# A decoder block in split single precision: two weight slabs of the projections exchange their ways of being multiplied, VectorE writes the diagonal matrices of the norms, and the FFN output's activations are split pair by pair

## The chip, the cores and the metric

The kernel runs on one core of a Trainium2 chip. The time is the device time of one execution in microseconds (us). Three runs of the kernel before took 939.85 us in the median (938.61 to 940.29). A further execution was recorded by the hardware profiler: it took 939.93 us, and its trace spans 937.8 us, so that 2.1 us lie around the span.

The five engines that matter are TensorE (PE in the profile, with PEld for its weight loads), VectorE (DVE), ScalarE (ACT), GpSimd (POOL) and SyncE (SP), which issues the transfers of the weights. Each carries out its own instructions in the order in which they stand in its queue; semaphores hold an instruction back until what it reads has been written and what it overwrites has been read.

## The reference

The input is x, 512 tokens of 1024 channels, with 16 meta tokens set before them (528 in all). Cut to its steps:

```python
u = rmsnorm(h, mix_norm_w)
q, k, v, g_ret, lru_in, lru_gate, gate_a, gate_b = split(u @ w_in)   # 1024 -> 8192
o = chunk_retention(rotary(q), rotary(k) * 128**-0.5, v)             # 8 heads of 128
o = o * rsqrt(mean(o * o) + eps)
y_ret = (silu(g_ret) * o) @ w_branch_ret
y_lru = (gelu(lru_gate) * rg_lru(conv(lru_in))) @ w_branch_lru
h = h + (sigmoid(gate_a) * y_ret + sigmoid(gate_b) * y_lru) @ w_out
u = rmsnorm(h, ffn_norm_w)
g, up = split(u @ w_ffn_in)                                          # 1024 -> 2 x 2816
h = h + (silu(g) * up) @ w_ffn_out                                   # 2816 -> 1024
return rmsnorm(h, final_norm_w)[:, 16:]
```

## The kernel before

All activations lie in SBUF; the weights are streamed from HBM once, in quarters ("pieces") of 128x512 numbers. Products are made in single precision from two halves: ScalarE casts a piece to `hi` (line 290), VectorE, for some pieces GpSimd, subtracts it from the piece and has `lo` (line 294, `low`). A product is three matmuls, hi x hi, hi x lo and lo x hi (lines 360 to 364, and 372 to 374 in `block`). Activations are split in the same way (`split`, lines 418 to 422: cast on line 421, subtraction on line 422).

A slab of weights (1024 input channels by 256 outputs) is multiplied in one of two ways. "Plain" takes eight blocks of twelve matmuls straight from the four pieces. "The scheme" (`fast`, lines 376 to 400) takes seven blocks, from pieces and from four sums of pieces that GpSimd makes (`combine`, lines 257 to 261: s1, s3, s2, s4, with the addition on line 260). So it casts and subtracts seven operands instead of four, and between its blocks it needs copies of PSUM by ScalarE (`ws` line 392, `pz` 394, `u2` 398) and one addition by VectorE (`pz` line 393), on whose result a later block on the same bank waits; at the end VectorE adds the parts (lines 407 and 408, for keys line 813). `PLAIN_R` (line 68) lists which slabs of queries (Q), keys (K) and ret gates (G) of the four pairs of heads, 0 to 3, are plain. In the trace the banks of a scheme carry its name: `zwg` and `yxg` are the two banks of a ret gate, `zwf` and `yxf` of an FFN input slab, `zwq` and `yxq` of a query slab; plain ones are named by the slab alone (`k`, `f`).

Pieces live in rings: 8 raw quarters (`RAW`), 4 sums (`SUMS`), 9 pairs hi and lo (`RING`). A piece is loaded when a slot is free.

Before each of the two large projections the rows are normed and transposed. `rms_factors` (lines 480 to 491) takes the mean square of a tile of 128 tokens (ScalarE, line 484), adds the epsilon (`rv`, GpSimd, line 476), raises it to the power -1/2 (`rr`, GpSimd, line 477) and writes the factor onto the diagonal of a 128x128 matrix (line 490, on GpSimd before the change). TensorE multiplies the tile with this diagonal (line 523), which norms and transposes it at once. The first norm has the tiles x0 to x3 (banks `uT`), the second the tiles h0 to h3 (banks `hT`); h0 and h1 go without a diagonal, by a row scale of VectorE (line 1123). VectorE then multiplies by the norm's weights (line 508), ScalarE casts (511), VectorE subtracts (513).

The first norm's order on the engines is written out by hand (`FIRST_STEPS`, lines 47 to 49). Everywhere else a scheduler in the compiler decides the order on each engine from its own model of durations; what the program states first has the higher priority. `behind` (line 239) adds an edge of order without a semaphore: with it each `combine` stays behind the diagonal last written on GpSimd.

The FFN has 22 slabs of input (`w_fi`, two plain, then a loop from `FIRST` to `NJ` with `fast512` and the gate `ffn_gate`), whose gated outputs are kept in `F`, eleven tiles of 128x1024, two slabs in each. The output projection (`w_fo`) walks over k = 0 to 21 and both halves of the outputs, with eight banks `fo`. `operand(i)` splits `F[i]`; before the change it is defined behind the input loop and is called for three tiles ahead at each k.

Of the kernel before, what the change touches and what calls it, by code (L numbers as in the profile page):

```python
# [11 lines left out]
F32R = mybir.dt.float32r  # L12
# [52 lines left out]

PLAN = "R0 R1 R2 R3 A0 A1 A2 A3 I0 I1 BR T0 L0 I2 T1 L1 I3 L2 T2 B0 L3 T3 B1 B2 B3 BL"

PLAIN_R = "K0 G0 K1 K2 K3".split()
NORM = 2.0
SUM = 2.0  # L70

# [39 lines left out]
class Slots:  # L111
# [28 lines left out]
    def put(self, *tiles):  # L140
        for t in tiles:
            _, slot, i = self.held.pop(id(t))
            if i is None:
                self.free.append(slot)
                continue
            slot[2] -= 1
            self.halves.append((slot, i))
            if slot[2] == 0:
                self.halves = [h for h in self.halves if h[0] is not slot]
                self.free.append(slot[0])  # L150
# [3 lines left out]
def hybrid_block(ctx: ExitStack, tc: tile.TileContext, a: dict):  # L154
# [84 lines left out]
    def behind(ins, other):  # L239

        if other is not None:
            tc.add_manual_dep(ins.ins, other.ins.name, mybir.DependencyInfo(
                mybir.DependencyClass.NoSync, mybir.DependencyReason.DATA), reason="issue order")
        return ins
# [12 lines left out]

    def combine(key, i, name, x, y, op):
        sums[key, i, name] = wpool.tile([P, Q4], F32, tag="sum", bufs=SUMS, name=f"{name}_{key}{i}")
        behind(nc.gpsimd.tensor_tensor(sums[key, i, name], x, y, op=op), state.get("diag"))  # L260
        return sums[key, i, name]

    def emit(n, later=False):
# [155 lines left out]
    def split(p, src, engine=nc.vector):  # L419
        hi, lo = p  # L420
        nc.scalar.copy(hi, src)  # L421
        engine.tensor_tensor(lo, src, hi.bitcast(F32), op=ALU.subtract)
# [57 lines left out]
    def rms_factors(src, name, parts=P, diagonal=True):  # L480

        scratch = get(D)
        ssq = small.tile([P, 1], F32, tag="ssq", bufs=4, name=f"ssq_{name}")
        nc.scalar.activation(scratch[:parts], src, AF.Square, accum_out=ssq[:parts])
        put(scratch)
        r = rsqrt_mean(ssq[:parts], D, 1, name, parts, engine=nc.gpsimd)
        if not diagonal:
            return r
        diag = get(P)
        state["diag"] = nc.gpsimd.tensor_scalar_mul(diag[:parts, :parts], ident[:parts, :parts], r)  # L490
        return diag


# [690 lines left out]
    token_half(1)  # L1184
    finish(item)
    put(*VX.pop("b12"))
    for j in range(FIRST, NJ):
        gu = get(D)
        fast512("w_fi", j, VV, gu, "f")
        ffn_gate(j, gu[:, :SEQ], gu[:, SEQ:])  # L1190
        for b in ("t1", "t3", "b21", "b11", "b22", "t4", "t2") if j == NJ - 1 else ():
            put(*VX.pop(b))
        put(gu)
# [40 lines left out]


    acc = [[bank(f"fo{t}_{hf}") for hf in range(2)] for t in range(NC_)]
    parts = {}

    def operand(i):

        if i < len(F) and i not in parts:
            parts[i] = get(D, F32R), get(D, F32R)
            split(parts[i], F[i])
            put(F[i])

    def token_tile(t, k, hf, w, start, stop):
        fh, fl = (p[:, k % 2 * SEQ + t * C:k % 2 * SEQ + (t + 1) * C] for p in parts[k // 2])
        mm3(acc[t][hf], fh, fl, *w, start, stop)

    ws = {}  # L1250
    for k in range(NJ - LAST_K):
        for i in range(k // 2, k // 2 + 3):
            operand(i)
        for hf in range(2):
            ws[k, hf] = weights(("w_fo", k // 2, k % 2 + 2 * (1 - hf)))[0]
            for t in range(NC_):
                token_tile(t, k, hf, ws[k, hf], k == 0, False)
        if k % 2 == 1:
            put(*parts.pop(k // 2))
    ks = range(NJ - LAST_K, NJ)  # L1260
# [71 lines left out]
```

## Time and profile before

| | us |
|---|---|
| median of 3 runs | 939.85 |
| profiled execution | 939.93 |
| its span | 937.8 |
| TensorE busy | 918.5 |
| VectorE busy | 681.3 |
| ScalarE busy | 464.4 |
| GpSimd busy | 343.0 |

TensorE is the engine to read first. Matmuls overlap in the trace: one of 256 columns is listed with some 0.28 us, but the next starts 0.12 us after it, so stretches are read by the starts. "Idle before" in square brackets at the end of a row is how long the engine stood still before the instruction, with what released it. [...]

### The profile page before, as it was taken

Reading aid. Unit: us, or ns where it says so; the run is one execution under the profiler, and the core shown is the slowest. Engines: PE = TensorE matmul, PEld = TensorE weight load, DVE = VectorE, ACT = ScalarE, POOL = GpSimd, SP = SyncE. Lnnn points to the kernel's source line nnn. Section 1 sums busy time; section 2 is a strip of 40 time slices with the busy share of each in tenths; the row PEclk is TensorE's granted clock in tenths of the full one; section 3 lists DMA queues with packets and bytes.
Section 4 is the critical chain, followed back from the end, with each engine's and each line's share of the span. In section 5 each row is a group of like instructions: output and inputs, shape, how many; then the busy total and the mean of one; then the engine's idle time right before and its main releaser. Section 6 shows DMA issues by size and latency. Waiting matters only on the chain.

```text
span 937.8 us, 16991 instructions
## 1 busy us (share of the span) xinstructions
PE 918.5 (98%) x6598; PEld 862.8 (92%) x6598; DVE 681.3 (73%) x912; ACT 464.4 (50%) x823; POOL 343.0 (37%) x247
## 2 busy tenths in 40 slices
PE   8999999999999999999999999999999999999996
PEld 8999999998999889999998888999999999788885
DVE  5877977888788836777745428999999999832223
ACT  6653454554555336847833314655555556722213
POOL 5234634445350002102200215587887885000003
PEclk9999999999999999999999999999999999999998
DMA  7142123131224332233442222132333234422202
GB/s 278 46 135 84 54 95 109 38 111 50 64 87 129 113 102 82 77 113 101 136 135 91 94 75 89 52 118 93 101 107 121 91 100 127 143 92 96 84 1 90
DMA packets 48496, 91.48 MB, mean 98 GB/s; under 512 B 5520, under 2 KB 5648, under 8 KB 48416
## 3 DMA queue, kind: packets, MB, share of 16 engines
q1 hardware_dynamic: 46976, 86.70, 28.6%
q10 hardware_dynamic: 1440, 3.71, 1.2%
q8 instruction: 51, 0.84, 0.3%
q14 instruction: 29, 0.24, 0.1%
HBM read 88.29 MB, written 2.10 MB: 96 GB/s over the span
## 4 chain that ended last, share of the span: by engine, by line
PE 90%; DVE 5%; DMA 2%; issue 2%; ACT 1%; POOL 1%; POOLq 0%; DVEq 0%; SPq 0%; ACTq 0%
PE fo L362 4%; PE fo L364 4%; PE fo L363 4%; PE zwf L372 4%; PE zwf L373 4%; PE zwf L374 4%; DVE lo L294 3%; PE yxf L372 3%; PE yxf L374 3%; PE yxf L373 3%; PE lg L374 2%; PE gate L374 2%; PE gate L372 2%; PE lg L372 2%; PE lg L373 2%
## 5 line engine op out<-in xcount | busy, mean ns | idle before, releaser
L294 DVE TENSOR_TENSOR lo<-raw_w_in,hi 128x512 fp32r<-128x512 f32 x99 | 84.7, 861 | 36.9 <-ACT hi L290 34.8
L372 PE MATMUL zwf<-b,hi 128*128 128x256 f32 x320 | 90.8, 285 | 1.8 <-DVE pzf L393 1.8
L290 ACT CAST hi<-raw_w_in 128x512 fp32r<-128x512 f32 x99 | 60.7, 620 | 63.8 <-PE w_br L363 13.8
L373 PE MATMUL zwf<-b,hi 128*128 128x256 f32 x320 | 89.6, 280 | 0.0
L374 PE MATMUL zwf<-b,lo 128*128 128x256 f32 x320 | 89.5, 280 | 0.0
L294 DVE TENSOR_TENSOR lo<-s_w_fi,hi 128x512 fp32r<-128x512 f32 x80 | 83.7, 1083 | 1.3 <-ACT hi L290 0.8
L294 DVE TENSOR_TENSOR lo<-raw_w_fo,hi 128x512 fp32r<-128x512 f32 x44 | 30.3, 690 | 64.7 <-ACT hi L290 64.7
L260 POOL TENSOR_TENSOR s_w_fi<-raw_w_fi,raw_w_fi 128x512 f32<-128x512 f32 x40 | 69.0, 1743 | 8.2 <-DVE lo L294 8.2
L362 PE MATMUL fo<-hi,b 128*128 128x512 f32 x176 | 69.6, 395 | 0.4 <-ACT b L421 0.4
L363 PE MATMUL fo<-lo,b 128*128 128x512 f32 x176 | 69.1, 393 | 0.0
L364 PE MATMUL fo<-hi,b 128*128 128x512 f32 x176 | 68.1, 393 | 0.0
L294 DVE TENSOR_TENSOR lo<-raw_w_fi,hi 128x512 fp32r<-128x512 f32 x46 | 67.7, 1500 | 0.0
L372 PE MATMUL yxf<-b,hi 128*128 128x256 f32 x240 | 65.5, 281 | 2.1 <-ACT pzf L394 2.1
L374 PE MATMUL yxf<-b,lo 128*128 128x256 f32 x240 | 66.7, 281 | 0.0
L373 PE MATMUL yxf<-b,hi 128*128 128x256 f32 x240 | 66.6, 280 | 0.0
L372 PEld LDWEIGHTS zwf<-b,hi 128*128 128x128 f32 x320 | 60.0, 188 | 4.3 <-DVE pzf L393 4.1
L290 ACT CAST hi<-raw_w_fo 128x512 fp32r<-128x512 f32 x44 | 27.3, 621 | 73.1 <-PE fo L364 71.4
L294 DVE TENSOR_TENSOR lo<-s_w_in,hi 128x512 fp32r<-128x512 f32 x52 | 50.6, 976 | 14.4 <-ACT hi L290 12.1
L374 PEld LDWEIGHTS zwf<-b,lo 128*128 128x128 f32 x320 | 60.4, 189 | 0.0
L373 PEld LDWEIGHTS zwf<-b,hi 128*128 128x128 f32 x320 | 60.3, 189 | 0.0
L290 ACT CAST hi<-s_w_fi 128x512 fp32r<-128x512 f32 x80 | 48.1, 617 | 20.8 <-PE zwf L373 15.0
L290 ACT CAST hi<-raw_w_fi 128x512 fp32r<-128x512 f32 x68 | 41.6, 619 | 33.0 <-PE yxf L373 18.2
(380 smaller groups left out, 3277.2 us busy)
## 6 DMA issues: line engine op xcount, KB each, us to landing
raw_w_in<-in_w_in SPq DMA_DIRECT2D x112, 256.0 KB, 3.1
raw_w_fi<-in_w_fi SPq DMA_DIRECT2D x88, 256.0 KB, 3.3
raw_w_fo<-in_w_fo SPq DMA_DIRECT2D x44, 256.0 KB, 2.9
raw_w_v<-in_w_v SPq DMA_DIRECT2D x16, 256.0 KB, 4.3
raw_w_br<-in_w_br SPq DMA_DIRECT2D x16, 256.0 KB, 3.3
raw_w_bl<-in_w_bl SPq DMA_DIRECT2D x16, 256.0 KB, 3.1
raw_w_out<-in_w_out SPq DMA_DIRECT2D x16, 256.0 KB, 2.9
b<-in_x SPq DMA_DIRECT2D x4, 512.0 KB, 6.3
```

Of the source, the lines that this page charges most:

```text
L260: behind(nc.gpsimd.tensor_tensor(sums[key, i, name], x, y, op=op), state.get("diag"))
L290: nc.scalar.copy(hi, src)
L294: engine.tensor_tensor(lo, src, hi.bitcast(F32), op=ALU.subtract)
L362: nc.tensor.matmul(out, wh, xh, start=start, stop=False, skip_group_check=True)
L363: nc.tensor.matmul(out, wh, xl, start=False, stop=False, skip_group_check=True)
L364: nc.tensor.matmul(out, wl, xh, start=False, stop=stop, skip_group_check=True)
L372: nc.tensor.matmul(out, wh, xh, start=start and i == 0, stop=False, skip_group_check=True)
L373: nc.tensor.matmul(out, wh, xl, start=False, stop=False, skip_group_check=True)
L374: nc.tensor.matmul(out, wl, xh, start=False, stop=i == 3, skip_group_check=True)
```

## The change

`PLAIN_R` takes the keys of pair 2 off the list and puts the ret gate of pair 3 on it: K2 (264 columns per block) goes from plain to the scheme, G3 (256 columns) from the scheme to plain. The diagonal of `rms_factors` is written by VectorE, and the edge of order between diagonals and sums is gone. `operand` is defined ahead of the FFN input loop; the tile 0 is split before the last input slab is stated, the others behind the first half of each k, one at a time, and two tiles ahead of their use at most.

```diff
-PLAIN_R = "K0 G0 K1 K2 K3".split()
+PLAIN_R = "K0 G0 K1 K3 G3".split()
...
-        behind(nc.gpsimd.tensor_tensor(sums[key, i, name], x, y, op=op), state.get("diag"))
+        nc.gpsimd.tensor_tensor(sums[key, i, name], x, y, op=op)
...
-        state["diag"] = nc.gpsimd.tensor_scalar_mul(diag[:parts, :parts], ident[:parts, :parts], r)
+        nc.vector.tensor_scalar_mul(diag[:parts, :parts], ident[:parts, :parts], r)
...
+    parts = {}
+    def operand(i):
+        if i < NJ // 2 and i not in parts:
+            parts[i] = get(D, F32R), get(D, F32R)
+            split(parts[i], F[i])
+            put(F[i])
     for j in range(FIRST, NJ):
+        if j == NJ - 1:
+            operand(0)
         gu = get(D)
         fast512("w_fi", j, VV, gu, "f")
...
     for k in range(NJ - LAST_K):
-        for i in range(k // 2, k // 2 + 3):
-            operand(i)
         for hf in range(2):
             ws[k, hf] = weights(("w_fo", k // 2, k % 2 + 2 * (1 - hf)))[0]
             for t in range(NC_):
                 token_tile(t, k, hf, ws[k, hf], k == 0, False)
+            if hf == 0:
+                operand((k + 1) // 2 + 1)
```

How the change moves instructions is shown at three places, before and after, by the order in which they stand in an engine's queue.

The first place is VectorE at the start of the program. `lo4` and `lo5` are weight pieces of the values, `uT1` and `uT2` the transposed tiles x1 and x2, `b20` the diagonal. Before:

```order
L294 TENSOR_TENSOR lo2_182<-raw_w_v0_2_128,hi2_181 128x512
L508 TENSOR_TENSOR b7_111<-uT1_1_202,vec_70 128x4x128
L508 TENSOR_TENSOR b6_110<-uT1_0_207,vec_70 128x4x128
L513 TENSOR_TENSOR b13_117<-b7_111,b12_116 128x4x128
L513 TENSOR_TENSOR b11_115<-b6_110,b10_114 128x4x128
L294 TENSOR_TENSOR lo4_264<-raw_w_v0_1_261,hi4_263 128x512
L294 TENSOR_TENSOR lo5_270<-raw_w_v1_1_267,hi5_269 128x512
```

With the change:

```order
L294 TENSOR_TENSOR lo2_182<-raw_w_v0_2_128,hi2_181 128x512
L490 TENSOR_SCALAR b20_148<-ident_82,rr_x2_198 128x128
L508 TENSOR_TENSOR b7_111<-uT1_1_202,vec_70 128x4x128
L508 TENSOR_TENSOR b6_110<-uT1_0_207,vec_70 128x4x128
L513 TENSOR_TENSOR b13_117<-b7_111,b12_116 128x4x128
L513 TENSOR_TENSOR b11_115<-b6_110,b10_114 128x4x128
L490 TENSOR_SCALAR b20_148<-ident_82,rr_x3_247 128x128
L294 TENSOR_TENSOR lo4_264<-raw_w_v0_1_261,hi4_263 128x512
L294 TENSOR_TENSOR lo5_270<-raw_w_v1_1_267,hi5_269 128x512
```

Two diagonals stand in the queue now: that of x2 (`rr_x2`) ahead of the two multiplications of tile x1, that of x3 ahead of `lo4` and `lo5`.

The second place is GpSimd at the second norm, around the factor of h3 (`rv_h3`, `rr_h3`). `s1_w_fi2` to `s4_w_fi2` are the sums of FFN input slab 2, `s1_w_fi3` the first of slab 3, `lo232` and `lo236` pieces of the plain slabs 0 and 1. Before:

```order
L294 TENSOR_TENSOR lo232_6681<-raw_w_fi0_1_6678,hi232_6680 128x512
L294 TENSOR_TENSOR lo236_6733<-raw_w_fi1_1_6730,hi236_6732 128x512
L476 TENSOR_SCALAR rv_h3_6743<-ssq_h3_6741 128x1
L477 TENSOR_TENSOR rr_h3_6744<-rv_h3_6743,mhalf_78 128x1
L490 TENSOR_SCALAR b176_6747<-ident_82,rr_h3_6744 128x128
L260 TENSOR_TENSOR s1_w_fi2_6753<-raw_w_fi2_0_6749,raw_w_fi2_1_6751 128x512
L260 TENSOR_TENSOR s3_w_fi2_6757<-raw_w_fi2_2_6755,raw_w_fi2_0_6749 128x512
L260 TENSOR_TENSOR s2_w_fi2_6759<-s1_w_fi2_6753,raw_w_fi2_2_6755 128x512
```

With the change:

```order
L294 TENSOR_TENSOR lo232_6675<-raw_w_fi0_1_6672,hi232_6674 128x512
L260 TENSOR_TENSOR s1_w_fi2_6747<-raw_w_fi2_0_6743,raw_w_fi2_1_6745 128x512
L294 TENSOR_TENSOR lo236_6727<-raw_w_fi1_1_6724,hi236_6726 128x512
L260 TENSOR_TENSOR s3_w_fi2_6751<-raw_w_fi2_2_6749,raw_w_fi2_0_6743 128x512
L260 TENSOR_TENSOR s2_w_fi2_6753<-s1_w_fi2_6747,raw_w_fi2_2_6749 128x512
L476 TENSOR_SCALAR rv_h3_6737<-ssq_h3_6735 128x1
L260 TENSOR_TENSOR s4_w_fi2_6757<-raw_w_fi2_3_6755,s2_w_fi2_6753 128x512
L260 TENSOR_TENSOR s1_w_fi3_7014<-raw_w_fi3_0_7010,raw_w_fi3_1_7012 128x512
L477 TENSOR_TENSOR rr_h3_6738<-rv_h3_6737,mhalf_78 128x1
```

Before, the factor of h3 and its diagonal stand directly behind the two `lo` and ahead of all sums; now the four sums of slab 2 and the first of slab 3 stand ahead of `rr_h3`. On TensorE the order there is the same in both: the transposes `hT2`, 24 matmuls of `f0`, then `hT3`, which reads the diagonal of h3.

The third place is the passage from the last FFN input slab (21) to the output, on TensorE. `yxf21` is a bank of that slab, `zwf21` the other. Before, the end of one block of `yxf21` and the start of the next, which reads the sum s2 (`hi376`) and follows on the same bank once ScalarE has copied it (`pzf21`, line 394):

```order
L372 MATMUL yxf21_9746<-b161_6353,hi373_9653 128x256
L373 MATMUL yxf21_9746<-b162_6354,hi373_9653 128x256
L374 MATMUL yxf21_9746<-b161_6353,lo373_9654 128x256
L372 MATMUL yxf21_9746<-b181_6947,hi376_9704 128x256
L373 MATMUL yxf21_9746<-b182_6948,hi376_9704 128x256
```

With the change:

```order
L372 MATMUL yxf21_9744<-b161_6347,hi373_9647 128x256
L373 MATMUL yxf21_9744<-b162_6348,hi373_9647 128x256
L374 MATMUL yxf21_9744<-b161_6347,lo373_9648 128x256
L362 MATMUL fo0_0_9884<-hi377_9716,b215_9738 128x512
L363 MATMUL fo0_0_9884<-lo377_9717,b215_9738 128x512
L364 MATMUL fo0_0_9884<-hi377_9716,b216_9739 128x512
```

Behind the block that ends with `lo373`, 29 matmuls of the output (`fo0_0` to `fo3_0`, and some of `fo0_1` and `fo1_1`) stand now, ahead of the next block of `zwf21`. The operand they read, `b215` and `b216`, is `F[0]`. On ScalarE the cast of `F[0]` (line 421, out of `b183`) has moved too. Before:

```order
L394 COPY pzf21_9748<-yxf21_9746 128x256
L320 ACTIVATE b214_9741<-b213_9615 128x512
L421 CAST b235_10434<-b211_9470 128x1024
L290 CAST hi383_9845<-raw_w_fo1_3_9843 128x512
L421 CAST b231_10282<-b205_8900 128x1024
L398 COPY u2f21_9749<-yxf21_9746 128x256
L290 CAST hi384_9863<-raw_w_fo1_1_9861 128x512
L421 CAST b217_9894<-b183_6960 128x1024
```

With the change:

```order
L290 CAST hi369_9556<-s2_w_fi20_9439 128x512
L421 CAST b215_9738<-b183_6954 128x1024
L290 CAST hi370_9588<-s1_w_fi21_9576 128x512
L392 COPY wsf20_9612<-zwf20_9610 128x256
L290 CAST hi371_9615<-s3_w_fi21_9580 128x512
L290 CAST hi372_9631<-raw_w_fi21_3_9584 128x512
```

`b217<-b183` (before) and `b215<-b183` (now) are the cast of `F[0]`. Before, it comes behind the last slab's `pzf21` and `u2f21` and behind casts of other tiles of `F`; now it comes ahead of the first operand of the last slab, `hi370`. On TensorE the waiting block of `yxf21` is no longer the next in the queue.

## Rows read from the trace of the kernel before

**Rows 1.** The page's head and its first part: the span, and each engine's busy time, its share and its number of instructions.

```profile
span 937.8 us, 16991 instructions
...
PE 918.5 (98%) x6598; PEld 862.8 (92%) x6598; DVE 681.3 (73%) x912; ACT 464.4 (50%) x823; POOL 343.0 (37%) x247
```

**Rows 2.** All waits of TensorE, grouped: what waited, for whose result, in total, how often, and the longest. Groups that are not used are left out.

```profile
PE uT L523 <- POOL b L490: 2.7, 1, 2.7
PE zwg L372 <- DVE pzg L393: 2.2, 1, 2.2
PE yxf L372 <- ACT pzf L394: 2.1, 2, 1.9
PE zwf L372 <- DVE pzf L393: 1.8, 3, 0.8
...
PE v L363 <- DVE lo L294: 0.7, 1, 0.7
...
PE fo L362 <- ACT b L421: 0.4, 1, 0.4
```

**Rows 3.** TensorE's timeline around the ret gate of pair 3: start, duration, engine, line, operation, number; in brackets the idle time before it and what ended it.

```profile
220.47 0.28 PE L374 MATMUL yxg<-b,lo 128*128 128x256 f32 x1
222.98 0.58 PE L372 MATMUL zwg<-b,hi 128*128 128x256 f32 x1 [2.23 <-DVE pzg L393]
```

**Rows 4.** Seven stretches of the span. Columns: from and to, length, then the busy us (and the number of instructions) of PE, PEld, DVE, ACT and POOL, the granted clock of TensorE, the share of the DMA engines' time and GB/s. They lie in the start, in the time of K2 (two stretches), behind the gate of pair 3 (three), and at the FFN's passage.

```profile
8.00:10.00 2.00, 1.87 (x9) 1.87 (x9) 0.00 (x0) 1.84 (x4) 0.83 (x3) 0.50 1.05 326
155.00:165.00 10.00, 10.00 (x86) 9.99 (x86) 6.58 (x9) 4.54 (x10) 3.86 (x3) 1.00 0.34 112
165.00:175.00 10.00, 10.00 (x84) 9.74 (x82) 8.40 (x12) 4.96 (x9) 3.67 (x2) 1.00 0.09 28
222.00:224.00 2.00, 1.02 (x5) 1.03 (x6) 2.00 (x6) 0.00 (x0) 0.37 (x2) 0.70 0.15 40
224.00:226.00 2.00, 2.00 (x11) 2.00 (x11) 1.50 (x2) 0.22 (x1) 0.95 (x1) 0.50 0.31 102
226.00:228.00 2.00, 2.00 (x15) 1.74 (x15) 0.69 (x1) 0.91 (x2) 0.74 (x1) 0.95 0.41 127
802.00:804.00 2.00, 0.61 (x5) 0.61 (x6) 2.00 (x4) 2.00 (x5) 0.00 (x0) 1.00 0.37 116
```

**Rows 5.** VectorE's timeline ahead of TensorE's wait at the gate of pair 3.

```profile
216.93 2.21 DVE L647 TENSOR_TENSOR b<-b,b 128x1056 f32<-128x1056 f32 x1
219.07 3.52 DVE L294 TENSOR_TENSOR lo<-raw_w_in,hi 128x512 fp32r<-128x512 f32 x2
222.51 0.41 DVE L393 TENSOR_TENSOR pzg<-zwg,wsg 128x256 f32<-128x256 f32 x1
```

**Rows 6.** VectorE's groups by line, the shapes kept apart: a multiplication of the keys' rotation over 128x1024, and a copy of 128x128.

```profile
L646 DVE TENSOR_TENSOR b<-b,b 128x1024 f32<-128x1024 f32 x4 | 4.9, 1224 | 3.5 <-ACT b L645 3.5
...
L885 DVE COPY b<-u 128x128 f32<-128x128 f32 x8 | 2.3, 285 | 2.0 <-PE u L883 2.0
```

**Rows 7.** TensorE's timeline at the second norm (the last matmul of `f0`, behind which `hT3` comes) and at the FFN's passage.

```profile
580.87 0.28 PE L374 MATMUL f<-b,lo 128*128 128x256 f32 x1
...
801.26 0.28 PE L374 MATMUL yxf<-b,lo 128*128 128x256 f32 x1
803.39 0.39 PE L372 MATMUL yxf<-b,hi 128*128 128x256 f32 x1 [1.86 <-ACT pzf L394]
```

**Rows 8.** ScalarE's timeline at the FFN's passage.

```profile
801.52 0.61 ACT L290 CAST hi<-raw_w_fo 128x512 fp32r<-128x512 f32 x1
802.04 1.04 ACT L421 CAST b<-b 128x1024 fp32r<-128x1024 f32 x1
802.98 0.36 ACT L394 COPY pzf<-yxf 128x256 f32<-128x256 f32 x1
```

**Rows 9.** GpSimd's timeline in the start: the factors of x2 and x3, and the diagonal of x3.

```profile
14.75 0.90 POOL L477 TENSOR_TENSOR rr_x<-rv_x,mhalf 128x1 f32<-128x1 f32 x1
...
18.48 0.57 POOL L477 TENSOR_TENSOR rr_x<-rv_x,mhalf 128x1 f32<-128x1 f32 x1
```

**Rows 10.** VectorE's timeline in the start.

```profile
15.14 1.28 DVE L508 TENSOR_TENSOR b<-uT,vec 128x512 f32<-128x512 f32 x2
...
18.66 1.29 DVE L294 TENSOR_TENSOR lo<-raw_w_v,hi 128x512 fp32r<-128x512 f32 x2 [0.86 <-DMA raw_w_in<-in_w_in]
```

**Rows 11.** GpSimd's timeline: one sum in the third pair's time, then the second norm from the first `lo` on.

```profile
214.04 1.28 POOL L260 TENSOR_TENSOR s_w_in<-raw_w_in,raw_w_in 128x512 f32<-128x512 f32 x1
...
574.74 1.61 POOL L294 TENSOR_TENSOR lo<-raw_w_fi,hi 128x512 fp32r<-128x512 f32 x1 [0.45 <-ACT hi L290]
...
579.37 0.19 POOL L476 TENSOR_SCALAR rv_h<-ssq_h 128x1 f32<-128x1 f32 x1 [0.73 <-ACT b L484]
579.65 0.57 POOL L477 TENSOR_TENSOR rr_h<-rv_h,mhalf 128x1 f32<-128x1 f32 x1
580.32 0.61 POOL L490 TENSOR_SCALAR b<-ident,rr_h 128x128 f32<-128x128 f32 x1
...
587.95 1.74 POOL L260 TENSOR_TENSOR s_w_fi<-raw_w_fi,raw_w_fi 128x512 f32<-128x512 f32 x1
```

**Rows 12.** SyncE's queue: the issue of a piece of FFN input slab 2.

```profile
573.92 0.33 SPq L255 DMA_DIRECT2D raw_w_fi<-in_w_fi  x1
```

**Rows 13.** The page's part on transfers: count, KB each, median us from issue to landing.

```profile
raw_w_fi<-in_w_fi SPq DMA_DIRECT2D x88, 256.0 KB, 3.3
```

More of the change, by code (lines that the diff above doesn't have):

```diff
@@ L1236, in hybrid_block @@
     acc = [[bank(f"fo{t}_{hf}") for hf in range(2)] for t in range(NC_)]
[L1237 to L1244, printed above, removed]
     def token_tile(t, k, hf, w, start, stop):
```

## The prediction, made before the run

> **What bounds the kernel now.** The page's head comes first [rows 1]: TensorE is busy for 918.5 of 937.8 us, 98%, and no other engine above 73%. So the time can change in two ways only: TensorE's work grows or shrinks, or its few waits and the stretches of low clock behind them do. The work stays: the gate of pair 3 gets an eighth block and the keys of pair 2 lose one, and the number of matmuls elsewhere is the same. What is left is the list of TensorE's waits [rows 2], second to be read. It has four entries near 2 us, and each lies at a place that the change touches or stands close to one: `uT`, for a diagonal of GpSimd; `zwg`, for VectorE's `pzg`; `yxf`, for ScalarE's `pzf`; `zwf`, three times, for VectorE. [...]
>
> The profiled execution took 939.93 us, 2.1 more than its span; the median of the runs is 939.85. I make the sum against 939.93; the 0.08 between them is nothing here.
>
> **Part one: G3 plain, K2 in the scheme.** In a plain slab nothing comes back from VectorE between the blocks, so the wait of `zwg` goes. TensorE's last matmul before it starts at 220.47 and the next at 222.98 [rows 3]; without the wait the next would come 0.12 later, so 2.4 us of idle time go. Behind it TensorE runs 1 us in the window with the mean of 0.70 and 2 us at 0.50; half of these 3 us is lost, about 1.5. Together 3.9 us. Bounds: 2.2, the wait alone, if another wait brings the low clock at another place, and 3.9.
>
> What K2 costs: three more `lo` of 0.65 (two take 1.29 [rows 10]), one `pz` of 0.41 [rows 5], and a multiplication of the whole slab of 1.22 where the plain form had it in parts [rows 6], 3.6 us of VectorE in all, four sums on GpSimd of 1.28 [rows 11] and a few copies on ScalarE. In the 20 us in which K2 runs, VectorE is busy for 6.6 + 8.4 = 15.0 us and GpSimd for 7.5, and TensorE never waits [rows 4]. With 18.6 of 20 us VectorE still keeps up on the mean. So I cost it at nothing; what covers it is 1.4 us of VectorE's free time. If the queue is in the wrong order the cover is gone, and then it is the wait of `zwg` over again (second rival). Term: -3.9.
>
> **Part two: the FFN's passage.** TensorE's matmul starts at 801.26 and the next at 803.39 [rows 7]: 2.0 us beyond the usual 0.12. The wait is for `pzf`, which ScalarE carries out at 802.98, directly behind a cast of a weight piece and a cast of a tile of `F`, 1.04 us long [rows 8]. So it is ScalarE's queue, filled by the casts of `F`, that is late. With the change, 29 matmuls of the output stand between the two blocks; their operand `F[0]` is cast ahead of the last slab's pieces. At 0.23 us each, by the columns (512 against 256 at 0.12), they are 6.7 us of work, more than the wait. The wait of `fo` for the cast of `F[0]`, 0.4 [rows 2] and 0.6 with its edges, goes with it. Term: -2.6. Bounds: -1.5, if the pieces of `w_fo` that these matmuls need are late on VectorE, which is busy for all of the window [rows 4], and -2.9.
>
> **Part three: the diagonals in the start.** The trace shows no diagonal on VectorE; by its copy of 128x128, 0.29 us [rows 6], I take 0.3. The wait of `uT` ends about 0.5 sooner, since the diagonal took GpSimd longer. But VectorE now waits in its queue for GpSimd's factors. The factor of x2 is done at 14.75 + 0.90 = 15.65 [rows 9], and behind its diagonal stand the two multiplications of tile x1, which started at 15.14 [rows 10]: 0.8 later. Their results are what ScalarE casts ahead of the square of x3, so the factor of x3 moves from 18.48 + 0.57 = 19.05 to some 19.8, its diagonal ends at 20.1, and behind it stand `lo4` and `lo5`, which started at 18.66 [rows 10]. So VectorE is 1.4 us late there. From here to the `lo` for which TensorE waited 0.7 us [rows 2] it has no free time, so that wait grows by about 1.3. The 0.5 won at `uT` is swallowed by it, because TensorE only comes to this wait sooner. Term: +1.3. Bounds: -0.5, if VectorE catches up, and +2.8, with 1.5 more for a clock that falls as at the gate.
>
> **Part four: the diagonals in the second norm.** This is the largest term. TensorE ends `f0` at about 581.0 and `hT3` follows with no wait, because the diagonal of h3 is done just then: factor at 579.65 to 580.22, diagonal from 580.32 [rows 7, 11]. With the change the sums of slabs 2 and 3 are no longer held behind the diagonal, and the order on GpSimd shows the scheduler has put them ahead of the factor: from `lo232`, which began at 574.74, there come s1, `lo236`, s3, s2, the epsilon, s4, the next slab's s1, and only then the power. s1 needs a piece whose transfer is issued at 573.92 [rows 12] and lands 3.3 later [rows 13], at 577.2. From there six operations of 128x512 stand ahead of the power, which with the epsilon takes 0.8 [rows 11], then 0.3 for the diagonal. A sum of this size took 1.28 us in one place and 1.74 in another [rows 11]. With 1.28 for all: 577.2 + 7.7 + 1.1 = 586.0, a wait of 5.0. With 1.74: 588.7, a wait of 7.7. Below the first I get only if the piece is early (`lo232` ends at 576.35): 4.1. I take 1.6 for the first three, beside VectorE's work, and 1.28 for the other three, because VectorE itself then stands waiting at the diagonal: 577.2 + 4.8 + 3.8 + 1.1 = 586.9, a wait of 6.0.
>
> [...]
>
> The wait is longer than that of the gate, so I add the same loss of clock, 1.5 [rows 4], between 0 as at 802 and twice as much. `hT3` is moved past nothing on TensorE, so nothing can fill the hole: 7.5. What is given back: during the wait VectorE and GpSimd get ahead, and of the three waits of `zwf` for VectorE, 1.8 in all [rows 2], the first may go: -0.5, between -1.8 and +0.5. That GpSimd no longer writes six diagonals, 0.6 us or more each [rows 11], is worth nothing where TensorE doesn't wait.
>
> **The sum.** 939.93 - 3.9 - 2.6 + 1.3 + 7.5 - 0.5 = 941.7.
>
> **The rivals.** *First, faster or at least not slower: the hole at `hT3` stays small.* The order on GpSimd is fixed, but the sums can be short and the clock may stay up, as it did at 802. Wait 5.0 without a loss of clock: 941.7 - 2.5 = 939.2. With the piece early and the lead paid back at all three `zwf`: 4.1 - 1.8 instead of 7.5 - 0.5, 937.0; with a start that costs nothing, 935.7. It decides from a wait of about 3 us at `hT3` on. Against it: six operations can't be undercut, and five of them depend on nothing that comes sooner. *Second, slower: K2 takes over the wait that G3 loses.* Its `pz` stands in VectorE's queue among `lo`s, and if more than 1.4 us too much work stands ahead of it, TensorE waits there as it did at `zwg`, 2.4 and the clock: 941.7 + 3.9 = 945.6. For it: at the gate it took only one multiplication of 2.21 and two `lo` of 3.52 together [rows 5]. Against it: the windows of K2 show no wait and free time. *Third, slower: the start's hole brings the low clock.* TensorE is at 0.50 already in 8 to 10 [rows 4]; a wait of 2 us at 25 could bring it back: +1.5, 943.2. *Fourth: the passage's matmuls wait for their own pieces*, and part two gives only the wait of `fo`: 941.7 + 2.0 = 943.7.
>
> **Chances.** My forecast 0.45, with its own range of 939.5 to 944; the first rival 0.27, the second 0.13, the third 0.08, the fourth 0.07. The measurement can't tell 0.2%, 1.9 us, from no change: faster is below 938.0, slower above 941.7. The forecast lies on that edge, so half of its chance is slower and half is the same. Faster has most of the first rival, 0.20, and a little of the forecast's tail, 0.03; slower has half of the forecast, the second rival and most of the others, 0.46; the same is left with 0.31. Two in ten outside gives 936.0 to 946.0.
>
> **What would show it.** In the list of waits: `zwg` and `yxf` gone; a new line, `hT` for VectorE's diagonal, of 5 to 7.7 us; `v` for VectorE's `lo` at 2 instead of 0.7; no line of `zk`. In the windows: the clock at 1.00 from 220 to 228, and low somewhere in the 4 us behind the new wait. I am wrong if GpSimd's `rr_h` of h3 starts before 584, if a wait on `pzk` appears, or if `fo` waits ahead of the last block of `zwf`.

## The result, and the profile after

The changed kernel took 943.77 us (median of 6 runs), the kernel before on the same chips 940.07: a ratio of 1.0039, with a 95% interval of 1.0029 to 1.005. It is slower by 3.7 us. The profiled execution spans 942.4 us, 4.6 more than that of before.

The head of the page of the changed kernel, against [rows 1]:

```profile
span 942.4 us, 16988 instructions
...
PE 919.7 (98%) x6598; PEld 864.1 (92%) x6598; DVE 671.4 (71%) x917; ACT 463.2 (49%) x818; POOL 334.5 (35%) x241
```

TensorE is busy for 1.2 us more, in a span that is 4.6 longer: the work has hardly changed, the holes have. The list of TensorE's waits, against [rows 2] (columns as there):

```profile
PE hT L523 <- issue: 6.8, 1, 6.8
PE uT L523 <- DVE b L490: 2.9, 2, 2.1
PE v L362 <- ACT hi L290: 1.5, 1, 1.5
PE warm L185 <- POOL ident masks.py:199: 1.4, 1, 1.4
PE o L895 <- DVE b L887: 1.3, 3, 0.9
PE zwf L372 <- DVE pzf L393: 0.6, 1, 0.6
PE v L363 <- DVE lo L294: 0.4, 1, 0.4
...
```

`zwg` is gone, and so are the 1.9 of `yxf` and the wait of `fo`. New are `hT`, 6.8 us at one place, `v` for ScalarE's `hi`, and a second wait of `uT`. (The trace names no releaser for `hT`, "issue"; that it is the diagonal is read from the engines below.) No wait of `zk` is there.

Where the time went is seen best when the same matmul is looked up in both timelines. Starts in us, and the difference:

| TensorE's matmul | before | after | difference |
|---|---|---|---|
| 97th of the values `v` | 30.58 | 33.26 | +2.7 |
| 17th of the scores `s` | 139.52 | 143.20 | +3.7 |
| first gate of the mixing (`zwgate`) | 230.06 | 230.19 | +0.1 |
| last of `f0` before `hT3` | 580.87 | 581.14 | +0.3 |
| first of `f` behind `hT3` | 582.79 | 591.65 | +8.9 |
| 96th of `f` | 591.22 | 600.74 | +9.5 |
| 301st of `zwf` | 664.18 | 671.59 | +7.4 |
| 101st of `fo`, behind the passage | 831.58 | 836.02 | +4.4 |
| last of `fo` | 930.33 | 934.95 | +4.6 |

So the start lost 2.7, then another 1.0 up to 140 us (the 0.5 more that an `o` waits for VectorE is half of it); the gate of pair 3 gave 3.6 back; the second norm lost 9.2; 2.1 of it came back in the 70 us behind it; the passage gave 3.0.

The hole at the second norm, first in GpSimd's timeline of the changed kernel, against [rows 11]: the sums of slab 2, a `lo` among them, the epsilon `rv`, s4, the next slab's s1, and last the power `rr`.

```profile
577.48 1.54 POOL L260 TENSOR_TENSOR s_w_fi<-raw_w_fi,raw_w_fi 128x512 f32<-128x512 f32 x1 [0.75 <-DMA raw_w_fi<-in_w_fi]
578.98 1.74 POOL L294 TENSOR_TENSOR lo<-raw_w_fi,hi 128x512 fp32r<-128x512 f32 x1
580.67 1.81 POOL L260 TENSOR_TENSOR s_w_fi<-raw_w_fi,raw_w_fi 128x512 f32<-128x512 f32 x1
582.45 1.71 POOL L260 TENSOR_TENSOR s_w_fi<-s_w_fi,raw_w_fi 128x512 f32<-128x512 f32 x1
584.24 0.51 POOL L476 TENSOR_SCALAR rv_h<-ssq_h 128x1 f32<-128x1 f32 x1
584.83 1.26 POOL L260 TENSOR_TENSOR s_w_fi<-raw_w_fi,s_w_fi 128x512 f32<-128x512 f32 x1
586.05 1.26 POOL L260 TENSOR_TENSOR s_w_fi<-raw_w_fi,raw_w_fi 128x512 f32<-128x512 f32 x1
587.27 0.55 POOL L477 TENSOR_TENSOR rr_h<-rv_h,mhalf 128x1 f32<-128x1 f32 x1
```

The power of h3 begins at 587.27; before, it began at 579.65. VectorE had nothing else to do at the end; its timeline shows the last two subtractions of the norm and then the diagonal, 3.15 us idle ahead of it:

```profile
581.28 3.41 DVE L513 TENSOR_TENSOR b<-b,b 128x512 fp32r<-128x512 f32 x2
587.85 0.29 DVE L490 TENSOR_SCALAR b<-ident,rr_h 128x128 f32<-128x128 f32 x1 [3.15 <-POOL rr_h L477]
```

TensorE's granted clock, a share of full speed, in the four windows behind (columns as in [rows 4]):

```profile
586.00:588.00 2.00, 0.00 (x0) 0.00 (x0) 0.15 (x1) 0.00 (x0) 1.82 (x3) 0.57 0.00 0
588.00:590.00 2.00, 1.76 (x8) 1.79 (x9) 0.14 (x1) 0.00 (x0) 0.00 (x0) 0.50 0.00 0
590.00:592.00 2.00, 2.00 (x11) 2.00 (x10) 1.64 (x2) 0.62 (x1) 0.00 (x0) 0.50 0.00 0
592.00:594.00 2.00, 2.00 (x14) 2.00 (x14) 2.00 (x4) 1.54 (x2) 0.00 (x0) 0.73 0.00 0
```

TensorE stands still from 581.26 on (its last matmul and 0.12) to 588.24, 7.0 us, and then its granted clock is 0.50 for over 4 us. The wait has a second price here, as at the gate before (0.70, then 0.50 [rows 4]).

The start is in VectorE's timeline, four diagonals (line 490) and the two `lo` behind the last, against [rows 10]:

```profile
6.71 0.28 DVE L490 TENSOR_SCALAR b<-ident,rr_x 128x128 f32<-128x128 f32 x1 [6.71 <-POOL rr_x L477]
...
10.26 1.28 DVE L490 TENSOR_SCALAR b<-ident,rr_x 128x128 f32<-128x128 f32 x1 [2.27 <-POOL rr_x L477]
...
16.26 0.29 DVE L490 TENSOR_SCALAR b<-ident,rr_x 128x128 f32<-128x128 f32 x1 [0.45 <-POOL rr_x L477]
...
20.41 1.30 DVE L490 TENSOR_SCALAR b<-ident,rr_x 128x128 f32<-128x128 f32 x1 [1.27 <-POOL rr_x L477]
21.62 3.46 DVE L294 TENSOR_TENSOR lo<-raw_w_v,hi 128x512 fp32r<-128x512 f32 x2
```

Two diagonals of the same size take 0.28 and 0.29 us, the other two 1.28 and 1.30; and `lo4` and `lo5`, 1.29 together before, take 3.46. GpSimd's timeline beside them:

```profile
10.20 1.26 POOL L294 TENSOR_TENSOR lo<-raw_w_v,hi 128x512 fp32r<-128x512 f32 x1
...
20.34 2.52 POOL L260 TENSOR_TENSOR s_w_in<-raw_w_in,raw_w_in 128x512 f32<-128x512 f32 x2
```

The two long diagonals begin 0.06 and 0.07 us behind the start of a GpSimd instruction of 128x512 and end just behind its end.

A part of the 2.7 us is the clock. In this execution it was low, 0.60 in the mean, while the first matmuls of `v` ran, from 12 to 16 us (the line below); in the trace of the kernel before it was at 1.00 there, and low earlier, 0.60 in 8 to 12:

```profile
12.00:16.00 4.00, 4.00 (x25) 4.00 (x25) 3.38 (x5) 2.71 (x5) 2.23 (x3) 0.60 1.05 408
```

The 25th and the 49th matmul of `v` are 1.1 us later than before; in the run of the diagonals alone (e3), with the same start and the clock at 1.00 there, they are 0.3 and 0.2 later. The other 1.6 us come between the 49th and the 97th, where TensorE waits for ScalarE's `hi` and VectorE's late `lo`; without the early fall TensorE would have come sooner and waited longer there, so that not all of the 1.1 is in the 2.7. What the clock did in the other runs is set out below, in "The clock in the start".

### The profile page after: what moved, and what is told of

It reads as the page before. It is cut to its first block, busy times and chain, and to the rows that moved or that the text cites. A ratio compares the mean times of both kernels' runs of the same rounds, so it can differ in the third digit from the quotient of the medians.

```text
span 942.4 us, 16988 instructions
## 1 busy us (share of the span) xinstructions
PE 919.7 (98%) x6598; PEld 864.1 (92%) x6598; DVE 671.4 (71%) x917; ACT 463.2 (49%) x818; POOL 334.5 (35%) x241
## 4 chain that ended last, share of the span: by engine, by line
PE 87%; DVE 6%; issue 3%; DMA 2%; ACT 1%; POOL 1%; POOLq 0%; DVEq 0%; ACTq 0%; SPq 0%
PE fo L364 4%; PE fo L362 4%; PE fo L363 4%; PE zwf L372 4%; PE zwf L373 4%; PE zwf L374 4%; PE yxf L374 3%; PE yxf L373 3%; PE yxf L372 3%; DVE lo L294 3%; PE lg L374 2%; PE gate L374 2%; PE gate L372 2%; PE lg L372 2%; PE lg L373 2%
## 5 line engine op out<-in xcount | busy, mean ns | idle before, releaser
L294 DVE TENSOR_TENSOR lo<-raw_w_in,hi 128x512 fp32r<-128x512 f32 x99 | 82.8, 845 | 32.1 <-ACT hi L290 31.9
L294 DVE TENSOR_TENSOR lo<-s_w_fi,hi 128x512 fp32r<-128x512 f32 x80 | 78.4, 1008 | 9.2 <-ACT hi L290 6.4
```

## The experiments

The first theory from the trace had five terms: the start +3 to +4, the gate -3.6, the passage -2.9, the hole +9.2, given back -2.2 (the passage and what is given back are 0.1 off: by the table they are -3.0 and -2.1). Four runs took the change apart.

**Sums behind the power (e1).** The changed kernel with one edge of order: each sum stays behind the last power of the norms. Lines in this and the next kernels shift by a few numbers.

```diff
-        nc.gpsimd.tensor_tensor(sums[key, i, name], x, y, op=op)
+        behind(nc.gpsimd.tensor_tensor(sums[key, i, name], x, y, op=op), state.get("diag"))
...
-        nc.gpsimd.tensor_tensor(r[:parts, :w], v[:parts, :w], mhalf[:parts, :w], op=ALU.pow)
+        power = nc.gpsimd.tensor_tensor(r[:parts, :w], v[:parts, :w], mhalf[:parts, :w], op=ALU.pow)
+        if name[0] in "xh":
+            state["diag"] = power
```

> The change, but with an edge of order that keeps the sums behind the last power of the norms on GpSimd; VectorE still writes the diagonals. First theory (the hole of 7.0 us ahead of hT3 is the power of h3 behind the sums in GpSimd's queue): no wait of hT above 1 us, clock 1.00 from 580 to 600; the 9.2 us lost there go, and the 2.2 us that were given back after it go too: 943.8 - 9.2 + 2.2 = 936.8, between 935.5 and 938. Rival (VectorE's own queue, the lo and the norm's subtractions ahead of the diagonal, holds it): the wait of hT stays at 3 us or more, time above 940. The start is unchanged by either: v 96 about 2.7 us later than before.

Measured: 939.0 us, 0.9989 of before (0.998 to 0.9999). The clock stayed at 1.00 from 580 to 592, so the bulk of the hole was the power behind the sums. But a wait of `hT` is left:

```profile
PE uT L525 <- DVE b L492: 2.9, 2, 1.9
PE hT L525 <- issue: 2.0, 1, 2.0
```

2.0 us is between the two expectations, and the time is over the upper bound. A part of that excess is in the start, which was expected unchanged: in this trace the 97th matmul of `v` (the expectations call it v 96) comes 4.0 us later than before instead of 2.7, because the clock fell to 0.68 behind the waits of `v`; in the changed kernel's trace it was 1.00 in the same window, from 28 to 32:

```profile
28.00:32.00 4.00, 3.83 (x22) 3.83 (x23) 3.80 (x7) 4.00 (x7) 0.72 (x2) 0.68 0.44 135
```

The other part is the wait of `hT`. VectorE's timeline of this run shows why it is left, three `lo` and then the diagonal of h3, with GpSimd's power and sums beneath:

```profile
575.61 4.07 DVE L294 TENSOR_TENSOR lo<-raw_w_fi,hi 128x512 fp32r<-128x512 f32 x3
...
582.78 1.28 DVE L492 TENSOR_SCALAR b<-ident,rr_h 128x128 f32<-128x128 f32 x1
```

```profile
581.83 0.55 POOL L477 TENSOR_TENSOR rr_h<-rv_h,mhalf 128x1 f32<-128x1 f32 x1
582.34 2.87 POOL L260 TENSOR_TENSOR s_w_fi<-raw_w_fi,raw_w_fi 128x512 f32<-128x512 f32 x2
```

The sums begin at 582.34, right behind the power, and the diagonal, which follows the same power, at 582.78 comes second and takes 1.28; in the changed kernel the same diagonal, with nothing behind the power on GpSimd, took 0.29. And the three `lo` took 4.07, where they took 2.99 before and in the changed kernel; two `lo` of GpSimd ran beside them, of 1.72 and 1.32, but two did so before as well, of 1.61 and 1.83, so that the 1.1 more is measured and its reason isn't shown. Behind them stands the addition (line 1151) whose sum ScalarE squares for the factor of h3, so that the power itself came late, at 581.83. The rival was right in a part: VectorE is late here on its own account, beside GpSimd's work.

**Diagonals back on GpSimd (e2)**, the other two parts kept.

```diff
-        nc.gpsimd.tensor_tensor(sums[key, i, name], x, y, op=op)
+        behind(nc.gpsimd.tensor_tensor(sums[key, i, name], x, y, op=op), state.get("diag"))
...
-        nc.vector.tensor_scalar_mul(diag[:parts, :parts], ident[:parts, :parts], r)
+        state["diag"] = nc.gpsimd.tensor_scalar_mul(diag[:parts, :parts], ident[:parts, :parts], r)
```

> Only the slabs and the split of the FFN operands are changed; the diagonals stay on GpSimd with the sums behind them. First theory (the whole loss comes from the diagonals): 940.07 - 3.6 (gate of pair 3) - 2.9 (passage) = 933.6, between 932.5 and 935, with the landmarks of before up to 160 us. Rival (K2 in the scheme or the stated order costs something that the head start after the hole hid): 936 or more, with a wait of zk or more waits of zwf than before.

Measured: 933.65 us, 0.9933 (0.9918 to 0.9948), as the first theory has it. No wait of `zk`, `zwg`, `hT` or `fo` is left. The three waits of `zwf` are there again, 1.8 us in all: they are what the lead behind the hole had paid back.

**Only the diagonals (e3)**, in the kernel before.

```diff
-        behind(nc.gpsimd.tensor_tensor(sums[key, i, name], x, y, op=op), state.get("diag"))
+        nc.gpsimd.tensor_tensor(sums[key, i, name], x, y, op=op)
...
-        state["diag"] = nc.gpsimd.tensor_scalar_mul(diag[:parts, :parts], ident[:parts, :parts], r)
+        nc.vector.tensor_scalar_mul(diag[:parts, :parts], ident[:parts, :parts], r)
```

> Before, with the diagonals on VectorE and the edge of order gone, nothing else. First theory: start + 3.2, hole and clock + 9.2, given back - 2.2 or less: 940.07 + 10 = 950, between 948.5 and 951.5, and the wait of zwg of 2 us still there. Rival (the loss needs the other parts, whose order has moved the sums): under 946.

Measured: 949.72 us, 1.0105 (1.009 to 1.012), as the first theory has it. The waits of `hT` (6.8), `zwg` (2.2) and `yxf` (2.1) stand side by side in its list. The parts don't need each other. In this execution the clock stayed at 1.00 behind the wait of `zwg` (224 to 228), where it had fallen in the kernel before, and fell behind that of `yxf` (0.65 and 0.50 from 812 to 816), where it had not.

**Only the FFN operands (e5).**

```diff
+        if j == NJ - 1:
+            operand(0)
...
-        for i in range(k // 2, k // 2 + 3):
-            operand(i)
...
+            if hf == 0:
+                operand((k + 1) // 2 + 1)
```

> Before, with the FFN operands split pair by pair, nothing else. First theory (the two waits at the passage go and nothing takes their place): 940.07 - 2.7 = 937.4, between 936.5 and 938.2. Rival (the casts are late anyway, the gain in the changed kernel came from the lead after the hole): 939 or more, with a wait of yxf or fo of over 1 us.

Measured: 937.0 us, 0.9971 (0.9958 to 0.9983); the waits of `fo` and of `yxf`, but for 0.3, are gone.

**Only the slabs (e4).**

```diff
-PLAIN_R = "K0 G0 K1 K2 K3".split()
+PLAIN_R = "K0 G0 K1 K3 G3".split()
```

> Before, with K2 in the scheme and G3 plain, nothing else. First theory: the wait of zwg and the low clock behind it go, nothing takes their place: 939.9 - 3.5 = 936.4, between 935.5 and 937.2; the waits of yxf (1.9) and fo (0.4) at the passage stay. Rival (K2 takes over the wait): 938.5 or more, with a wait of zk.

Measured: 937.47 us, 0.9978 (0.9969 to 0.9988): a gain of 2.2 where 3.5 was expected, no wait of `zk`. Its timeline is some 3.6 us ahead of that of before from 230 us to the passage, and only 2.6 us ahead behind it. The wait at the passage is the same as before (the line of the list of waits), but here the clock falls behind it (the window, columns as in [rows 4]):

```profile
PE yxf L372 <- ACT pzf L394: 2.1, 2, 1.9
```

```profile
800.00:815.00 15.00, 15.00 (x77) 13.23 (x77) 13.97 (x18) 10.33 (x15) 0.00 (x0) 0.89 0.30 96
```

In the kernel before, the window of the same wait had 1.00 [rows 4]. So in this execution 1.0 us was lost at the passage, which the edit doesn't touch. Whether the other executions lost it at the same place isn't shown.

What the start lost could have two causes. By the place, VectorE waits in its queue for factors that GpSimd has not yet made, and what stands behind is late. By what runs beside it (the expectations call this the theory of the port, after a reason that no run here shows), VectorE's diagonals and `lo`s take longer while GpSimd works, as the 1.28, 1.30 and 3.46 of the changed kernel did. Four runs, all built on the first experiment, tell them apart.

**Diagonals later in the hand-written order (e6).** In the first norm the factor is made at its old step, and the diagonal at a step of its own, `D`.

```diff
-FIRST_STEPS = ("F0 H L F1 T01 T00 W H P x01 H x00 h01 H l01 h00 l00 L P F2 T11 T10 x11 x10 h11 l11 h10 l10 v F3 T21 T20 "
-               "H L H L x21 x20 h21 l21 h20 l20 v H L T31 T30 H L v Fm x31 x30 h31 l31 h30 l30 Tm v xm").split()
+FIRST_STEPS = ("F0 D0 H L F1 T01 T00 W H P x01 D1 H x00 h01 H l01 h00 l00 L P F2 T11 T10 x11 x10 D2 h11 l11 h10 l10 v F3 T21 T20 "
+               "H L H L D3 x21 x20 h21 l21 h20 l20 v H L T31 T30 H L v Fm x31 x30 h31 l31 h30 l30 Tm v xm").split()
...
+            elif kind == "D":
+                factor, diags[int(t)] = diags[int(t)], get(P)
+                nc.vector.tensor_scalar_mul(diags[int(t)], ident, factor)
```

> e1 with the four diagonals of the first norm stated later in the hand-written order, where VectorE has work until the factor is there: that of x1 behind the first multiplication of x0, that of x2 behind those of x1, that of x3 behind lo4 and lo5. Theory of the place (VectorE waits in its queue for factors, and what stands behind is late): v 96 comes 0 to 1 us later than before, not 4; no wait of v for ScalarE's hi; 939.0 - 3.5 = 935.5, between 934.3 and 936.8. Theory of the port (the diagonals and lo beside GpSimd's sums are long wherever they stand): diagonals still at 1.28 and v 96 at +2.5 or more, 938 or more.

Measured: 934.59 us, 0.9939 (0.9924 to 0.9954). The 97th matmul of `v` comes 0.8 us before that of the kernel before, and no `v` waits. Yet the diagonals of x1 and x3 still take 1.28 and 1.30. So moving the diagonals is enough to win the loss back, with the long diagonals still there; `lo4` and `lo5`, now ahead of the diagonal of x3, take 2.39:

```profile
17.80 2.39 DVE L294 TENSOR_TENSOR lo<-raw_w_v,hi 128x512 fp32r<-128x512 f32 x2 [0.85 <-ACT hi L290]
20.12 1.30 DVE L783 TENSOR_SCALAR b<-ident,rr_x 128x128 f32<-128x128 f32 x1
```

**Sums behind the meta tokens' power (e7).** VectorE's order as in the first experiment; GpSimd is kept idle while VectorE writes the diagonal of x3 and subtracts.

```diff
-        if name[0] in "xh":
+        if name[0] in "xhm":
```

> e1 with the first slab's sums on GpSimd also held behind the power of the meta tokens' norm, so that GpSimd is idle while VectorE writes the diagonal of x3 and lo4, lo5; VectorE's order as in e1. Theory of the port: the diagonal of x3 takes 0.3 instead of 1.3, lo4 and lo5 together 1.3 instead of 3.47, the wait of v for hi of 1.5 goes, v 96 at +1.0 to +1.8 instead of +4.0; 939.0 - 2.5 = 936.5, between 935.3 and 937.6. Theory of the place: the wait for the factor of x3 stays and with it v 96 at +3 or more, 938.2 or more. If the sums, 9 us later, are late for the first scheme, zwq waits.

Measured: 934.17 us, 0.9935 (0.9919 to 0.9952). VectorE's diagonals of x1 and x3, and the two `lo`:

```profile
10.25 1.28 DVE L492 TENSOR_SCALAR b<-ident,rr_x 128x128 f32<-128x128 f32 x1 [2.37 <-POOL rr_x L477]
...
20.40 0.29 DVE L492 TENSOR_SCALAR b<-ident,rr_x 128x128 f32<-128x128 f32 x1 [1.28 <-POOL rr_x L477]
20.60 1.29 DVE L294 TENSOR_TENSOR lo<-raw_w_v,hi 128x512 fp32r<-128x512 f32 x2
```

The diagonal of x1, beside a `lo` of GpSimd, is long as ever; that of x3, now alone, takes 0.29, and the two `lo` 1.29 instead of 3.47. The wait for the factor of x3 is still there, 1.28 us of idle time, and costs nothing that TensorE sees: its 97th matmul of `v` comes 0.5 before that of the kernel before. The gain was larger than I had put it, 4.8 instead of 2.5; the clock has a part in it (see below).

**Both (e8)**, with the two edits above.

> e6 and e7 together. If place and port add, v 96 at 0 or below, and 939.0 - 4.0 = 935.0, between 933.8 and 936.3; if one of them alone makes the loss, the time is that of e6 or of e7.

Measured: 933.79 us, 0.9931 (0.9916 to 0.9946), at the lower edge of what was expected and within the noise of either alone. In its trace the 97th matmul of `v` comes 1.7 earlier than before, 0.9 ahead of the first run and 1.2 ahead of the second, but that isn't clear in the time. A likely reason, not tested further, is that both take the same collision away: the diagonal of x3 and `lo4`, `lo5` beside the first sums. So in these runs the loss of the start takes both, VectorE's order and GpSimd's work beside it, and either edit removes most of it (4.4 and 4.8 us against the 939.0 of e1).

**The unit matrix from PSUM (e9).** One diagonal, that of x1, reads the unit matrix from PSUM; nothing else is changed against the first experiment.

```diff
-        nc.vector.tensor_scalar_mul(diag[:parts, :parts], ident[:parts, :parts], r)
+        unit = pw[:, :P] if name == "x1" else ident[:parts, :parts]
+        nc.vector.tensor_scalar_mul(diag[:parts, :parts], unit, r)
```

> e1 with one thing changed: VectorE reads the unit matrix for the diagonal of x1 from its copy in PSUM that the warming matmuls leave there, not from SBUF. Theory of the port: this diagonal, which starts right behind the start of a lo on GpSimd, takes 0.2 to 0.4 instead of 1.28, and uT of x1 starts 0.9 sooner (wait of about 1 instead of 1.95). Theory of the place, or of a cost in VectorE itself: 1.28 still. Time 938.5, between 937.5 and 939.5, since VectorE is late again from the diagonal of x3 on.

Measured: 937.89 us, 0.998 (0.9969 to 0.9992). VectorE's diagonals of x1 and x3:

```profile
10.04 0.35 DVE L493 TENSOR_SCALAR b<-warm,rr_x 128x128 f32<-128x128 f32 x1 [2.25 <-POOL rr_x L477]
...
19.26 1.31 DVE L493 TENSOR_SCALAR b<-ident,rr_x 128x128 f32<-128x128 f32 x1 [1.28 <-POOL rr_x L477]
```

Beside the same GpSimd instruction the diagonal of x1 takes 0.35 instead of 1.28, and that of x3, which still reads SBUF, 1.31. TensorE's wait there falls from 1.95 to 1.29, and the 25th matmul of `v` comes 0.9 sooner than in the run of the diagonals alone (e3); in both traces the clock is at 1.00 from 8 to 16. So for this diagonal it is where the operand lies that makes the difference, since only that was changed: 1.28 out of SBUF, 0.35 out of PSUM. What in the chip holds the long one up is not seen in a trace.

**The clock in the start.** Read over these runs, the granted clock accounts for a part of what the start lost and won. The table has the granted clock in three windows and the starts of two matmuls of `v` against the kernel before:

| run | 8 to 12 | 12 to 16 | 28 to 32 | 25th of `v` | 97th of `v` |
|---|---|---|---|---|---|
| before | 0.60 | 1.00 | 1.00 | 0 | 0 |
| only the slabs (e4), start as before | 1.00 | 1.00 | 1.00 | -0.4 | -0.4 |
| diagonals on GpSimd (e2), start as before | 0.50 | 0.71 | 1.00 | +1.3 | +0.3 |
| the change | 1.00 | 0.60 | 1.00 | +1.1 | +2.7 |
| only the diagonals (e3), start as changed | 1.00 | 1.00 | 0.63 | +0.3 | +3.7 |
| sums behind the power (e1) | 1.00 | 0.57 | 0.68 | +1.0 | +4.0 |
| unit matrix from PSUM (e9) | 1.00 | 1.00 | 0.57 | -0.6 | +3.1 |
| diagonals later (e6) | 1.00 | 1.00 | 1.00 | -0.8 | -0.8 |
| sums behind meta (e7) | 1.00 | 1.00 | 1.00 | +0.5 | -0.5 |
| both (e8) | 0.57 | 1.00 | 1.00 | -0.7 | -1.7 |

The early fall comes in one execution of a start and not in another: compare the kernel before with e4 (0.60 and 1.00 in 8 to 12), and the change with e3 (0.60 and 1.00 in 12 to 16). The later matmuls make up for a part of it: in e2, 1.3 us at the 25th are 0.3 at the 97th. The late one stands behind TensorE's waits of `v` at 24 to 28, in e1 and in the change 1.5 us for `hi` and 0.4 for `lo`; of the four runs that have the wait for `hi`, three have it (0.68 in e1, 0.63 in e3, 0.57 in e9, against 1.00 in the change). From the 49th to the 97th matmul of `v`, e1 loses 3.0 us where the change loses 1.6, so the late fall cost 1.4 there. Of the 4.5 us at the 97th matmul by which e7 is ahead of e1, 1.4 are this fall, and up to 0.5, the lead at the 25th, the early one; so an estimate of what the collision cost is 2.6 to 3.1, near the 2.5 I had put. Over all executions the mean granted clock is 0.994 for e1, and 0.997 to 0.998 for e6 and e7, so that the clock differs not in one trace alone. In e7 the waits of `v` are 0.7 us in all, in e1 1.9; the median is 4.8 us lower, more than the waits' length.

**The mixed kernel (e10).** The first norm's diagonals on VectorE as in the run of both, those of h2 and h3 on GpSimd ahead of the sums.

```diff
-        nc.vector.tensor_scalar_mul(diag[:parts, :parts], ident[:parts, :parts], r)
+        state["diag"] = nc.gpsimd.tensor_scalar_mul(diag[:parts, :parts], ident[:parts, :parts], r)
```

> e8, with the diagonals of h2 and h3 on GpSimd again, ahead of the sums, and those of the first norm on VectorE as in e8. Theory of the port: in e8 the wait of hT of 2.0 comes from VectorE's diagonal of h3, 1.29 beside a sum, and from lo's beside GpSimd's; with the diagonal on GpSimd the wait is under 1 us: 933.8 - 1.5 = 932.3, between 931.3 and 933.2. Rival (the wait of hT is VectorE's late additions and not the diagonal): the wait of hT stays near 2 us and the time at 933.5 to 934.5.

Measured: 932.0 us, 0.9924 (0.9911 to 0.9937). It has the lowest median of this study, 11.8 us below the changed one; against e2 and e8 the intervals overlap. Its waits of TensorE:

```profile
PE uT L525 <- DVE b L783: 3.0, 2, 1.7
PE zwf L372 <- DVE pzf L393: 2.1, 3, 1.0
PE warm L185 <- POOL ident masks.py:199: 1.4, 1, 1.4
PE o L900 <- DVE b L892: 0.9, 3, 0.5
PE yxf L372 <- ACT pzf L394: 0.3, 1, 0.3
```

No `hT` is left. GpSimd's diagonal of h3 takes 0.61 and starts 0.67 us behind the start of the power; in e8 VectorE's took 1.29 and started 0.95 behind it:

```profile
574.66 0.61 POOL L492 TENSOR_SCALAR b<-ident,rr_h 128x128 f32<-128x128 f32 x1
```

The power too comes sooner, 1.6 us behind the first matmul of `f` instead of 2.8, and VectorE's three `lo` ahead of it take 2.99 instead of 4.07. The norm is not all of the gain: in the two traces e10 is 1.0 us ahead at its start already, and of the 2.0 us of the wait e8 wins 1.2 back behind it.

## Why the prediction was right, and where it was off

The forecast was 941.7, with a range of 936.0 to 946.0 and slower as the likeliest sign; 943.77 was measured. By the steps:

**G3 and K2, -3.9.** 3.6 in the timelines. Right against this trace: the wait and the low clock behind it went together, and K2 took over nothing; the second rival is out, since none of the runs with K2 in the scheme has a wait of `zk`. That the clock falls behind this wait is not sure: 0.70 and 0.50 in the kernel before [rows 4], but in e3 the same wait of 2.2 left it at 1.00.

**The passage, -2.6.** 3.0 in the timelines, 2.9 in the time of the run with that part alone. Right, and the fourth rival, that the passage's matmuls wait for their own pieces, is out: no wait of `fo` is in the list.

**The second norm, +7.5.** 9.2. The order of events was right, the power of h3 behind six operations of GpSimd: the first four took 1.54 to 1.81 beside VectorE's work, the last two 1.26, alone. The idle time was 7.0 where I had 6.0. The step that was too small is "I take 1.6 for the first three" and 1.28 for the rest. That an operation of GpSimd is longer beside VectorE's work was an assumption, and the 1.6 an estimate between the 1.28 and the 1.74 of [rows 11]; the changed kernel's trace shows four that meet VectorE's work, at 1.70 in the mean, and the epsilon takes longer too (0.51 instead of 0.19). The clock's fall, 1.5 by the gate, was 1.6 up to the first matmul of `f` and 0.7 more behind it. The first rival is out: the wait stayed long, and the clock fell.

**Given back, -0.5.** 2.1 came back, the waits of `zwf` at 609 and 651 and some more: 0.3 beyond the bound of -1.8. Two of the three waits went where I had one.

**The start, +1.3.** 2.7 to 3.7: this step failed in its size. I priced a diagonal on VectorE "by its copy of 128x128, 0.29 us" and took 0.3. That row is a copy out of PSUM; a diagonal reads the unit matrix out of SBUF, and two of four take 1.3 beside GpSimd's work. So the 0.5 that was to be won at `uT` went into a second wait: 0.8 and 2.1 us where there had been one of 2.7. The larger part is what hangs on the last diagonal: `lo4` and `lo5` start 3.0 us later than before where I had 1.4, fall under the first slab's sums and take 3.46 instead of 1.29. I had moved them as blocks with their old durations; here a step that was moved beside another engine's work did not keep its duration. By e3, whose start is the same and whose clock did not fall early, the start costs 3.7, less some 1.4 for its late fall of the clock: about 2.3, an estimate. The upper bound of 2.8 holds for that, and for the 97th matmul of `v`, but not for the 3.7 at 140 us.

**The third rival, the clock falling behind the start's wait, +1.5.** In the changed kernel's trace the clock stayed at 1.00 there, so the rival is no part of these 4.6 us. But such a fall came in e1, e3 and e9 (0.68, 0.63 and 0.57 from 28 to 32), and cost 1.4 in e1. Whether it came in the changed kernel's other executions isn't shown.

That the sum came out only 2 us too small is luck in part. The norm was 1.7 too small, and what comes back behind it 1.6 too small the other way, and these two cancel; so do the 0.3 of the gate and the 0.4 of the passage. What is left is the start.

Open is where the last 1.0 us between 33 and 140 us comes from. The start alone (e3: +3.7, then +3.6) and the slabs alone (e4: -0.4, then -0.2) don't lose it. With both, the runs go from 0.5 won (e7) to 1.0 lost (the change).

## What to carry to other kernels

An edge of order that seems to belong to an instruction one moves may be protecting another: here the edge "sums behind the diagonal" was what kept the power of the norm, which nobody touched, ahead of 8 us of GpSimd's sums, and it was lost with the diagonal. When work goes to an idle engine, read whose instructions will run beside it: an operation of 0.28 us took 1.3, and two `lo` that were pushed under GpSimd's sums took 2.2 more. And a part that gains (6 us by two of the parts) should be timed alone before the sum of all is judged. When two runs are compared by their traces, read the granted clock window by window first: of 4.5 us between two runs here, 1.4 to 1.9 were the clock.

## What the runs showed of the hardware that was not expected

A diagonal of 128x128 on VectorE took 0.27 to 0.29 us alone, 1.28 to 1.31 beside GpSimd's operations of 128x512 (in the changed kernel two began 0.06 and 0.07 behind the start of one of 1.26), and 0.35 in the one case where its operand lay in PSUM (e9). Two `lo` on VectorE took 1.29 alone (e7) and 3.46 beside GpSimd's sums (the changed kernel); and sums that take 1.26 alone took 1.54 to 1.81 beside VectorE's work at the second norm: both sides lose.

The same wait of 1.86 us at the FFN's passage left the clock at 1.00 in one run and was followed by a mean of 0.89 over 15 us in another (e4), at a cost of 1.0 us; in e3 it fell there too (0.65 and 0.50 from 812 to 816). The wait of `zwg` of 2.2 was followed by 0.70 and 0.50 in the kernel before and by 1.00 in e3. The wait of `hT` of 2.0 left it at 1.00 in e1. So in these traces a wait of 2 us came with a loss of clock in some executions and without one in others; behind the 6.8 us of the hole it came in both runs that had it, 0.50 in the windows behind.
